# Rotating the queries feature-major in two PSUM banks, in a two-layer trunk

## Chip, core and metric

One core of a Trainium2 chip runs the whole program. The metric is the device time of one execution in microseconds (us); the median of several runs counts.

## What is computed

A trunk of two layers on 512 positions and 1024 features, all fp32: a pooling mixer, then multi-head latent attention, then a final norm. The change lies in the second layer. Cut to that:

```
def apply_rope(t, cos, sin):
    half = QK_ROPE_DIM // 2                      # 32
    t1, t2 = t[..., :half], t[..., half:]
    return concatenate([t1 * cos - t2 * sin, t2 * cos + t1 * sin], axis=-1)

def mla_layer(...):                              # 16 heads
    proj = rmsnorm(x, norm_g) @ w_in             # q_lat 384, kv_lat 256, k_rope 64, z 2048
    q = (rmsnorm(q_lat, q_norm_g) @ w_q_b).reshape(B, S, 16, 192)
    q_nope, q_rope = q[..., :128], q[..., 128:]
    kv = (rmsnorm(kv_lat, kv_norm_g) @ w_kv_b).reshape(B, S, 16, 256)
    k_nope, v = kv[..., :128], kv[..., 128:]
    q_rope, k_rope = apply_rope(q_rope), apply_rope(k_rope)
    s = q_nope . k_nope + q_rope . k_rope        # causal, scaled
    y = (softmax(s) @ v).reshape(B, S, 2048) * silu(z)
    return x + y @ w_out
```

## The kernel before, in words

Products are made from three matmuls (`mm3`, lines 181 to 184): each operand is kept as a rounded half `hi` and a remainder `lo`. ACT copies into `hi`, DVE or POOL subtracts for `lo` (`halves`, line 186; `Strip.split`, line 164, for weights). Weights come through five `raw` buffers by transfers that SP issues (lines 154 and 160), are split, and stay in four large or two small strips. PSUM has eight banks, taken by `bank()`.

Attention runs over 16 heads. The queries' rotary part is made for four heads at a time, a *part*, by the class `QRope` (line 700). For one part, `a(t)` makes 128 positions: nine matmuls of 256 columns (positions on the partitions), the rotation by `rope` (line 645: four DVE instructions) and `halves` into `qs`, hi and lo side by side. `b(t)` turns that with four PE transposes (line 728), so that features lie on the partitions, and ACT copies it into `q_r` (line 733). The four `a` and `b` of a part are spread out by hand: part 0 between the gate projections (`gates`, line 739), the later ones one per head (lines 954 to 977).

A head's iteration (line 952) has, in order: `scores(h + 1)` (line 857), the transposes of head h's probabilities (line 900), the softmax of h + 1, two of the projection units of the next pair of heads (line 797: `k` and `q`, each with a copy of its first 128 positions at line 817), `b`, `values(h)` (line 915), `a`, and after an odd head the two `v` units. In scores, `q_r` is multiplied with `k_a` and `k_b` (lines 869, 870), the other part of query and key by `mm3`, for the first block in one fp32 matmul (line 872) that takes the copies `q` and `k` of line 817. DVE takes the maxima `mx` (line 876), scales them to `nm` (line 889), ACT makes the exponentials (line 892), DVE the reciprocal and the scaling (lines 895, 898). The program is not issued as written: a scheduler orders each engine's queue by the order in the program and by what it takes to be ready, except in the stages marked `manual_schedule`.

"Head h" below is the stretch on PE that begins with the transposes of head h; the scores at its end are those of h + 2. Its rows start at 569.83 us for head 8, 580.69 for head 9 and 594.55 for head 10.

Of the kernel before, what the change touches and what calls it, by code (L numbers as in the profile page):

```python
# [11 lines left out]
F32 = mybir.dt.float32  # L12
F32R = mybir.dt.float32r
I32 = mybir.dt.int32
AF = mybir.ActivationFunctionType
# [35 lines left out]
def trunk_kernel(  # L51
# [20 lines left out]
    def f32(ap):  # L72
        return ap.bitcast(F32)
# [19 lines left out]
    def bank(dtype=F32):  # L93
        return ps.tile([P, 512], dtype, name="bank", tag="bank")
# [75 lines left out]
    def strip(parts, eng=dve, small=False):  # L170
        st = Strip(parts, small=small)
        st.split(st.pieces, eng)
        return st.views
# [12 lines left out]
    def halves(src, hi, lo):  # L186
        act.activation(hi, src, AF.Copy)  # L187
        dve.tensor_tensor(lo, src, f32(hi), ALU.subtract)
# [456 lines left out]
    def rope(src, t, nh):  # L645
        shape = [P, nh, DR]
        hf = DR // 2
        o = lp.tile([P, 4, DR], F32, name="rope_o", tag="rope", bufs=3)[:, :nh, :]
        q = lp.tile([P, 4, DR], F32, name="rope_q", tag="rope", bufs=3)[:, :nh, :]
        cb = cs2[:, t, :].unsqueeze(1).to_broadcast(shape)  # L650
        dve.tensor_tensor(o, src, cb, ALU.mult)
        for a, b in ((0, hf), (hf, 0)):
            sb = sn2[:, t, a : a + hf].unsqueeze(1).to_broadcast([P, nh, hf])
            dve.tensor_tensor(q[:, :, a : a + hf], src[:, :, b : b + hf], sb, ALU.mult)
        dve.tensor_tensor(o, o, q, ALU.add)
        return o

    def latents():
        for t in range(NT):
            for c0, c in ((0, QR), (QR, KVR)):  # L660
                v = lat[:, t, c0 : c0 + c]
                junk = lp.tile([P, QR], F32, name="junk", tag="t2", bufs=2)
                rs = inv_rms(v, junk[:, :c], c)
                dve.tensor_scalar(v, v, rs, None, ALU.mult)

# [10 lines left out]

    def k_rope_a(t):
        o = rope(lat[:, t, QR + KVR :].unsqueeze(1), t, 1)
        kh = lt.tile([P, 2, DR], F32R, name="kh", tag="kr", bufs=8)
        kl = lt.tile([P, 2, DR], F32R, name="kl", tag="kr", bufs=8)  # L680
        halves(o.to_broadcast([P, 2, DR]), kh, kl)
        return kh, kl

# [13 lines left out]

    q_r = {}

    class QRope:  # L700


        def __init__(self, part):
            (self.wv,) = strip([(w_q[:, :, 4 * part : 4 * part + 4, DN:], 3, 256)], eng=pool, small=True)
            home = lp if part == 0 else wk
            self.out = home.tile([P, 4, S], F32R, name="q_r", tag="q_r", bufs=1 + (part > 0))
            q_r[part] = self.out
            self.q = {}

        def a(self, t):  # L710
            b = bank()[:, :256]
            for k in range(3):
                mm3(
                    b,
                    tuple(v[:, k, t * P : (t + 1) * P] for v in (latT_hi, latT_lo)),
                    tuple(v[:, k, :] for v in self.wv),
                    k == 0,
                    k == 2,
                )
            o = rope(b.rearrange("p (h c) -> p h c", h=4), t, 4)  # L720
            q = lp.tile([P, 4, 2, DR], F32R, name="qs", tag="t2", bufs=2)
            halves(o, q[:, :, 0, :], q[:, :, 1, :])
            self.q[t] = q

        def b(self, t):
            b = bank(F32R)
            for i in range(4):
                pe.transpose(  # L728
                    b[:, i * P : (i + 1) * P],
                    self.q[t][:, i].rearrange("p a c -> p (a c)"),  # L730
                    identr,
                )
            act.activation(
                self.out[:, :, t * P : (t + 1) * P],
                f32(b).rearrange("p (h c) -> p h c", h=4),
                AF.Copy,
            )

    def gates(s, between=()):
        (wv,) = strip([(w_cols(w_in2, LAT + s * 256, 256), KD, 256)])  # L740
# [7 lines left out]
    latents()  # L748
    gates(0)
    lat_rows()  # L750
    kk = [k_rope_a(t) for t in range(NT)]
    gates(1)
    k_rope_b(kk)
    qr = QRope(0)
    gates(2, [lambda: qr.a(0), lambda: qr.a(1)])
    qr.b(0)
    gates(3, [lambda: qr.a(2), lambda: qr.a(3)])
    qr.b(1)
    gates(4, [lambda: qr.b(2), lambda: qr.b(3)])
    for i in range(5, 8):  # L760
        gates(i)


# [174 lines left out]
    qr = {1: QRope(1)}  # L938
    k0()
    q0()  # L940
    qr[1].a(0)
    k1()
    sc = scores(0)
    softmax(*sc)
    q1()
    qr[1].a(1)
    for u in vs:
        u()
    qr[1].b(0)
    units = projections(1)  # L950
    fill = {12: [(0, 0)], 13: [(0, 1)], 14: [(1, 0), (1, 1)], 15: [(2, 0), (2, 1)]}
    for h in range(H):
        p, odd = divmod(h, 2)
        g, t = divmod(h + 6, 4)
        gb, tb = divmod(h + 5, 4)
        if h == min(fill):
            o2.load(0, y_late)
        nxt = scores(h + 1) if h + 1 < H else None
# [9 lines left out]
        for i, (t_, n) in enumerate(fill.get(h, ())):  # L968
            for j in range(2):
                o2.block(0, t_, n, j)  # L970
        if h < 11:
            qr[gb].b(tb)
        values(h)
        if g < 4:
            if t == 0:
                qr[g] = QRope(g)
            qr[g].a(t)
        if odd:
            for u in units[2]:
                u()  # L980
# [16 lines left out]
        ap.tile([P, D], F32, name="o", tag=tag, bufs=n)  # L997
        for tag, n in (("pm", 2), ("pm", 2), ("pt_hi", 1), ("pt_lo", 1))
    ]
    junk = lp.tile([P, 512], F32, name="junk", tag="t2", bufs=2)  # L1000
    ssq = {t: [] for t in range(NT)}
    rs = {}
    lefts, rights = slice(0, 512), slice(512, D)
# [109 lines left out]
```

## Time and profile before

| | |
|---|---|
| median of 3 runs | 743.92 us (742.78 to 744.31) |
| profiled execution | 742.62 us, span 740.8 us |
| PE | 726.3 us busy (98%), granted clock 0.997 |
| DVE, ACT, POOL | 386.2 (52%), 326.8 (44%), 95.3 us (13%) |
| transfers | 28.2% of 16 engines' span on SP's queue, 63.06 MB |

Busy times can overlap between engines and say nothing alone of what waits for what. A matmul's duration is a model and overlaps the next one's, so the distance between two starts tells what one costs. "Idle before" in brackets is the time an engine stood still ahead of an instruction, with what ended it.

### The profile page before, as it was taken

To read this page: it belongs to the slowest core of one execution; us is meant where nothing else is said; L and a number is where in the kernel's file an instruction comes from. 1 tells how busy PE (TensorE), PEld (TensorE's weight loads), DVE (VectorE), ACT (ScalarE), POOL (GpSimd) and SP (SyncE) were. 2 spreads that over 40 slices of the span, in tenths; PEclk is the share of its full clock that TensorE was granted. 3 is DMA by queue.
4 is the path that set the end of the run, shared out by engine and by line. 5 is a ranking of instruction groups with operands and counts; after the bars stand their busy time and mean duration, and the time that the engine had idled before them with its cause. 6 is when DMAs were issued, how large, how long until landed. Compare 5 with 4: busy or idle time off the path is not lost.

```text
span 740.8 us, 10219 instructions
## 1 busy us (share of the span) xinstructions
PE 726.3 (98%) x3747; PEld 622.4 (84%) x3747; DVE 386.2 (52%) x824; ACT 326.8 (44%) x749; POOL 95.3 (13%) x141
## 2 busy tenths in 40 slices
PE   7999999999999999999999999999999999999995
PEld 6888888888888888889888888989898989888884
DVE  5954444544655323271633312767776767744325
ACT  6552332322324322254633334675666565623314
POOL 5000000000000000234500014230232020000006
PEclk9999999999999999999999999999999999999998
DMA  7433233233233223224432313120121021113203
GB/s 258 127 116 95 76 114 98 75 112 114 71 100 114 88 85 109 70 78 112 136 102 58 108 51 113 37 77 10 37 86 48 4 71 58 58 58 114 82 19 113
DMA packets 58914, 63.91 MB, mean 86 GB/s; under 512 B 10736, under 2 KB 44656, under 8 KB 58864
## 3 DMA queue, kind: packets, MB, share of 16 engines
q1 hardware_dynamic: 58720, 63.06, 28.2%
q8 instruction: 29, 0.48, 0.3%
q14 instruction: 21, 0.17, 0.1%
q10 hardware_dynamic: 144, 0.20, 0.1%
HBM read 61.15 MB, written 2.10 MB: 85 GB/s over the span
## 4 chain that ended last, share of the span: by engine, by line
PE 94%; DVE 2%; ACT 1%; POOL 1%; issue 1%; DMA 0%; POOLq 0%; SPq 0%; ACTq 0%
PE bank L182 28%; PE bank L184 28%; PE bank L183 28%; PE bank L906 2%; PE bank L300 2%; PE bank L869 1%; PE bank L870 1%; DVE xn L217 1%; PE bank L728 1%; PE bank L872 1%; PE bank L928 0%; DMA xs<-in_x 0%; ACT xn L197 0%; DVE xs L572 0%; PE bank L270 0%
## 5 line engine op out<-in xcount | busy, mean ns | idle before, releaser
L166 ACT ACTIVATE w_hi<-raw 128x512 fp32r<-128x512 f32 (+2 forms) x240 | 127.4, 584 | 192.3 <-PE bank L183 181.4
L167 DVE TENSOR_TENSOR w_lo<-raw,w_hi 128x512 fp32r<-128x512 f32 x172 | 112.1, 690 | 171.8 <-ACT w_hi L166 169.9
L182 PE MATMUL bank<-h_hi,w_hi 128*128 128x512 f32 x368 | 143.7, 391 | 0.0
L184 PE MATMUL bank<-h_lo,w_hi 128*128 128x512 f32 x368 | 143.3, 389 | 0.0
L183 PE MATMUL bank<-h_hi,w_lo 128*128 128x512 f32 x368 | 143.2, 389 | 0.0
L167 POOL TENSOR_TENSOR w_lo<-raw,w_hi 128x256 fp32r<-128x256 f32 (+2 forms) x68 | 62.3, 946 | 311.0 <-ACT w_hi L166 310.8
L184 PEld LDWEIGHTS bank<-h_lo,w_hi 128*128 128x128 f32 x368 | 69.1, 188 | 14.4
L183 PEld LDWEIGHTS bank<-h_hi,w_lo 128*128 128x128 f32 x368 | 69.1, 188 | 14.1
L182 PEld LDWEIGHTS bank<-h_hi,w_hi 128*128 128x128 f32 x368 | 69.1, 188 | 14.1
L182 PE MATMUL bank<-w_hi,yh 128*128 128x512 f32 x128 | 49.9, 390 | 0.0
L184 PE MATMUL bank<-w_lo,yh 128*128 128x512 f32 x128 | 49.8, 389 | 0.0
L183 PE MATMUL bank<-w_hi,yl 128*128 128x512 f32 x128 | 49.8, 389 | 0.0
L876 DVE CUSTOM_DVE_ANT_0 pm<-bank,mask 128x128 f32<-128x128 f32 (+2 forms) x64 | 30.5, 490 | 15.8 <-PE bank L184 11.8
L892 ACT ACTIVATE pm<-pm,nm 128x128 f32<-128x128 f32 (+1 forms) x64 | 35.5, 564 | 1.8 <-DVE nm L889 1.3
L182 PE MATMUL bank<-w_hi,latT_hi 128*128 128x256 f32 x112 | 32.6, 291 | 0.0
L182 PE MATMUL bank<-latT_hi,w_hi 128*128 128x512 f32 x80 | 32.5, 406 | 0.0
L184 PE MATMUL bank<-w_lo,latT_hi 128*128 128x256 f32 x112 | 31.6, 282 | 0.0
L183 PE MATMUL bank<-w_hi,latT_lo 128*128 128x256 f32 x112 | 31.6, 282 | 0.0
L184 PE MATMUL bank<-latT_lo,w_hi 128*128 128x512 f32 x80 | 31.4, 392 | 0.0
L183 PE MATMUL bank<-latT_hi,w_lo 128*128 128x512 f32 x80 | 31.2, 390 | 0.0
L187 ACT ACTIVATE pt_hi<-bank 128x512 fp32r<-128x512 f32 (+2 forms) x48 | 20.0, 490 | 23.6 <-PE bank L906 23.6
L184 PEld LDWEIGHTS bank<-w_lo,yh 128*128 128x128 f32 x128 | 24.0, 188 | 5.0
(202 smaller groups left out, 1434.0 us busy)
## 6 DMA issues: line engine op xcount, KB each, us to landing
raw<-in_pool_w_in SPq DMA_DIRECT2D x64, 256.0 KB, 3.2
raw<-in_pool_w_out SPq DMA_DIRECT2D x32, 256.0 KB, 3.2
raw<-in_mla_w_in SPq DMA_DIRECT2D x32, 256.0 KB, 3.0
raw<-in_mla_w_out SPq DMA_DIRECT2D x32, 256.0 KB, 3.3
raw<-in_mla_w_q_b SPq DMA_DIRECT2D x36, 128.0 KB, 2.4
raw<-in_pool_w_group SPq DMA_DIRECT2D x16, 256.0 KB, 2.6
raw<-in_mla_w_kv_b SPq DMA_DIRECT2D x16, 256.0 KB, 3.0
raw<-in_mla_w_in SPq DMA_DIRECT2D x16, 176.0 KB, 2.7
```

Of the source, the lines that this page charges most:

```text
L166: act.activation(hi, raw, AF.Copy)
L167: ins = eng.tensor_tensor(lo, raw, f32(hi), ALU.subtract)
L182: pe.matmul(o, a[0], b[0], start=start, stop=False)
L183: pe.matmul(o, a[1], b[0], start=False, stop=False)
L184: pe.matmul(o, a[0], b[1], start=False, stop=stop)
L187: act.activation(hi, src, AF.Copy)
L217: dve.scalar_tensor_tensor(xn, xs[:, t, :], rs, g, ALU.mult, ALU.mult)
L300: pe.matmul(first[i][:, c], w0.views[0][a][:, k, i * P : (i + 1) * P], (h_hi, h_lo)[b][:, k, c], start=k == 0 and n == 0, stop=k == KD - 1 ...
L728: pe.transpose(b[:, i * P : (i + 1) * P], self.q[t][:, i].rearrange("p a c -> p (a c)"), identr,)
L876: dve.tensor_tensor_reduce(out=pm[:, OFF[i] : OFF[i] + w], in0=o[:, :w], in1=mask[:, S - w :], scale=1.0, scalar=-3.0e38, op0=ALU.add, op1 ...
L892: act.activation(v, v, AF.Exp, bias=nm[:, i : i + 1], scale=SCALE, accum_out=l[:, i : i + 1])
L906: pe.transpose(b[:, n : n + P], pm[:, OFF[i] + j * P : OFF[i] + (j + 1) * P], ident)
```

## The change

A part is now made feature-major. The weights' columns are put in the order half (2), head (4), feature (32) when they are split, the product `half(a)` has these columns as the stationary side and all 512 positions as the moving side, so one bank holds the first rotary half of four heads, another the second. `turn` rotates between the two banks with tables `cosT` and `sinT` (made once: two POOL copies, eight PE transposes, two ACT copies) and splits into `stack`. Sixteen transfers of 32 partitions x 512 put each head's four pieces (two halves, hi and lo) below one another in `q_r`. The transposes and ACT copies of `b` are gone. Part 0 has its halves in `gates(2)` and turns after it; part g = 1, 2, 3 has half 0 before head 0 or in heads 3 and 7, and half 1 and the turn in heads 0, 4 and 8. Several tiles have fewer buffers.

```diff
@@ -645,8 +645,8 @@
     def rope(src, t, nh):
         shape = [P, nh, DR]
         hf = DR // 2
-        o = lp.tile([P, 4, DR], F32, name="rope_o", tag="rope", bufs=3)[:, :nh, :]
-        q = lp.tile([P, 4, DR], F32, name="rope_q", tag="rope", bufs=3)[:, :nh, :]
+        o = lp.tile([P, 4, DR], F32, name="rope_o", tag="turned", bufs=1)[:, :nh, :]
+        q = lp.tile([P, 4, DR], F32, name="rope_q", tag="rope", bufs=1)[:, :nh, :]
         cb = cs2[:, t, :].unsqueeze(1).to_broadcast(shape)
         dve.tensor_tensor(o, src, cb, ALU.mult)
         for a, b in ((0, hf), (hf, 0)):
@@ -659,7 +659,7 @@
         for t in range(NT):
             for c0, c in ((0, QR), (QR, KVR)):
                 v = lat[:, t, c0 : c0 + c]
-                junk = lp.tile([P, QR], F32, name="junk", tag="t2", bufs=2)
+                junk = lp.tile([P, QR], F32, name="junk", tag="t2", bufs=1)
                 rs = inv_rms(v, junk[:, :c], c)
                 dve.tensor_scalar(v, v, rs, None, ALU.mult)
 
@@ -676,8 +676,7 @@
 
     def k_rope_a(t):
         o = rope(lat[:, t, QR + KVR :].unsqueeze(1), t, 1)
-        kh = lt.tile([P, 2, DR], F32R, name="kh", tag="kr", bufs=8)
-        kl = lt.tile([P, 2, DR], F32R, name="kl", tag="kr", bufs=8)
+        kh, kl = kr[:, 2 * t], kr[:, 2 * t + 1]
         halves(o.to_broadcast([P, 2, DR]), kh, kl)
         return kh, kl
 
@@ -697,44 +696,81 @@
 
     q_r = {}
 
+    cosT = lp.tile([P, S], F32, name="cosT")
+    sinT = lp.tile([P, S], F32, name="sinT")
+
+    def turned_tables():
+
+        four = lp.tile([P, 2, NT, 4, DR // 2], F32, name="four", tag="t2", bufs=1)
+        for i, (src, dst) in enumerate(
+            ((cs2[:, :, : DR // 2], cosT), (sn2[:, :, DR // 2 :], sinT))
+        ):
+            pool.tensor_copy(
+                four[:, i], src.unsqueeze(2).to_broadcast([P, NT, 4, DR // 2])
+            )
+            b = bank()
+            for t in range(NT):
+                pe.transpose(
+                    b[:, t * P : (t + 1) * P],
+                    four[:, i, t].rearrange("p h f -> p (h f)"),
+                    ident,
+                )
+            act.activation(dst, b, AF.Copy)
+
     class QRope:
 
 
         def __init__(self, part):
-            (self.wv,) = strip([(w_q[:, :, 4 * part : 4 * part + 4, DN:], 3, 256)], eng=pool, small=True)
-            home = lp if part == 0 else wk
-            self.out = home.tile([P, 4, S], F32R, name="q_r", tag="q_r", bufs=1 + (part > 0))
+            st = Strip([(w_q[:, :, 4 * part : 4 * part + 4, DN:], 3, 256)], small=True)
+
+            order = dict(a=2, h=4)
+            pieces = [
+                (
+                    raw[:, 0].rearrange("p (h a f) -> p h a f", **order),
+                    hi[:, 0].rearrange("p (a h f) -> p h a f", **order),
+                    lo[:, 0].rearrange("p (a h f) -> p h a f", **order),
+                )
+                for raw, hi, lo in st.pieces
+            ]
+            st.split(pieces, pool)
+            (self.wv,) = st.views
+            home = wk if part % 2 else lp
+            self.out = home.tile([P, 4, S], F32R, name="q_r", tag="q_r", bufs=1)
             q_r[part] = self.out
-            self.q = {}
-
-        def a(self, t):
-            b = bank()[:, :256]
+            self.banks = []
+
+        def half(self, a):
+            b = bank()
             for k in range(3):
                 mm3(
                     b,
-                    tuple(v[:, k, t * P : (t + 1) * P] for v in (latT_hi, latT_lo)),
-                    tuple(v[:, k, :] for v in self.wv),
+                    tuple(v[:, k, a * P : (a + 1) * P] for v in self.wv),
+                    tuple(v[:, k, :] for v in (latT_hi, latT_lo)),
                     k == 0,
                     k == 2,
                 )
-            o = rope(b.rearrange("p (h c) -> p h c", h=4), t, 4)
-            q = lp.tile([P, 4, 2, DR], F32R, name="qs", tag="t2", bufs=2)
-            halves(o, q[:, :, 0, :], q[:, :, 1, :])
-            self.q[t] = q
-
-        def b(self, t):
-            b = bank(F32R)
+            self.banks.append(b)
+
+        def turn(self):
+            one, two = self.banks
+            stack = lp.tile([P, 4, S], F32R, name="stack", tag="t2", bufs=1)
+            for n in range(2):
+                c = slice(n * 256, (n + 1) * 256)
+                o = lp.tile([P, 2, 256], F32, name="turned", tag="turned", bufs=1)
+                for i, (x, z, op) in enumerate(
+                    ((one, two, ALU.subtract), (two, one, ALU.add))
+                ):
+                    q = lp.tile([P, 256], F32, name="crossed", tag="rope", bufs=1)
+                    dve.tensor_tensor(o[:, i, :], x[:, c], cosT[:, c], ALU.mult)
+                    dve.tensor_tensor(q, z[:, c], sinT[:, c], ALU.mult)
+                    dve.tensor_tensor(o[:, i, :], o[:, i, :], q, op)
+                halves(o, stack[:, :2, c], stack[:, 2:, c])
             for i in range(4):
-                pe.transpose(
-                    b[:, i * P : (i + 1) * P],
-                    self.q[t][:, i].rearrange("p a c -> p (a c)"),
-                    identr,
-                )
-            act.activation(
-                self.out[:, :, t * P : (t + 1) * P],
-                f32(b).rearrange("p (h c) -> p h c", h=4),
-                AF.Copy,
-            )
+                for j in range(4):
+                    nc.sync.dma_start(
+                        f32(self.out[j * 32 : (j + 1) * 32, i, :]),
+                        f32(stack[i * 32 : (i + 1) * 32, j, :]),
+                    )
 
     def gates(s, between=()):
         (wv,) = strip([(w_cols(w_in2, LAT + s * 256, 256), KD, 256)])
@@ -748,16 +784,15 @@
     latents()
     gates(0)
     lat_rows()
+    kr = xn_tile(F32R).rearrange("p (n a c) -> p n a c", n=2 * NT, a=2)
     kk = [k_rope_a(t) for t in range(NT)]
+    turned_tables()
     gates(1)
     k_rope_b(kk)
     qr = QRope(0)
-    gates(2, [lambda: qr.a(0), lambda: qr.a(1)])
-    qr.b(0)
-    gates(3, [lambda: qr.a(2), lambda: qr.a(3)])
-    qr.b(1)
-    gates(4, [lambda: qr.b(2), lambda: qr.b(3)])
-    for i in range(5, 8):
+    gates(2, [lambda: qr.half(0), lambda: qr.half(1)])
+    qr.turn()
+    for i in range(3, 8):
         gates(i)
 
 
@@ -938,21 +973,18 @@
     qr = {1: QRope(1)}
     k0()
     q0()
-    qr[1].a(0)
     k1()
     sc = scores(0)
     softmax(*sc)
     q1()
-    qr[1].a(1)
+    qr[1].half(0)
     for u in vs:
         u()
-    qr[1].b(0)
     units = projections(1)
     fill = {12: [(0, 0)], 13: [(0, 1)], 14: [(1, 0), (1, 1)], 15: [(2, 0), (2, 1)]}
     for h in range(H):
         p, odd = divmod(h, 2)
-        g, t = divmod(h + 6, 4)
-        gb, tb = divmod(h + 5, 4)
+        g, t = divmod(h + 5, 4)
         if h == min(fill):
             o2.load(0, y_late)
         nxt = scores(h + 1) if h + 1 < H else None
@@ -968,13 +1000,13 @@
         for i, (t_, n) in enumerate(fill.get(h, ())):
             for j in range(2):
                 o2.block(0, t_, n, j)
-        if h < 11:
-            qr[gb].b(tb)
         values(h)
-        if g < 4:
+        if g < 4 and t < 2:
             if t == 0:
                 qr[g] = QRope(g)
-            qr[g].a(t)
+            qr[g].half(t)
+            if t == 1:
+                qr[g].turn()
         if odd:
             for u in units[2]:
                 u()
@@ -997,7 +1029,7 @@
         ap.tile([P, D], F32, name="o", tag=tag, bufs=n)
         for tag, n in (("pm", 2), ("pm", 2), ("pt_hi", 1), ("pt_lo", 1))
     ]
-    junk = lp.tile([P, 512], F32, name="junk", tag="t2", bufs=2)
+    junk = lp.tile([P, 512], F32, name="junk", tag="t2", bufs=1)
     ssq = {t: [] for t in range(NT)}
     rs = {}
     lefts, rights = slice(0, 512), slice(512, D)
```

On SP's queue the sixteen transfers of each part (line 770 of the changed kernel, `q_r<-stack`) stand among the loads of raw weights, which they used not to. From the first head on:

```order
+L770 DMA q_r<-stack 32x512 x16
+L154 DMA raw<-in_mla_w_q_b 128x4x64 x3
+L154 DMA raw<-in_mla_w_q_b 128x2x128 x3
+L160 DMA raw<-in_mla_w_kv_b 128x512 x2
+L154 DMA raw<-in_mla_w_q_b 128x2x128 x3
+L160 DMA raw<-in_mla_w_kv_b 128x512 x2
+L770 DMA q_r<-stack 32x512 x16
```

The `128x4x64` loads, the weights of the next part, come directly behind a part's transfers.

On PE, the end of head 2 (last matmul of its values, line 928, then scores of head 4). In the kernel before, from the last three matmuls of an `a` on:

```order
L182 MATMUL bank<-w_hi,latT_hi 128x256
L183 MATMUL bank<-w_hi,latT_lo 128x256
L184 MATMUL bank<-w_lo,latT_hi 128x256
L869 MATMUL bank<-k_a,q_r 128x256
L870 MATMUL bank<-k_b,q_r 128x256
L872 MATMUL bank<-k_4293,q_4309 128x128
L869 MATMUL bank<-k_a,q_r 128x384
L870 MATMUL bank<-k_b,q_r 128x384
L182 MATMUL bank<-kh,qh 128x384
```

In the changed one (lines 904, 905 and 907 are 869, 870 and 872 of before), where values and scores are adjacent:

```order
L963 MATMUL bank<-pt_3651,v_4155 128x128
L904 MATMUL bank<-k_a,q_r 128x256
L905 MATMUL bank<-k_b,q_r 128x256
L904 MATMUL bank<-k_a,q_r 128x384
L905 MATMUL bank<-k_b,q_r 128x384
L182 MATMUL bank<-kh,qh 128x384
L907 MATMUL bank<-k_4227,q_4243 128x128
L183 MATMUL bank<-kh,ql 128x384
```

Three matmuls of the third block moved ahead of the one that takes the copy `q`; heads 6 and 10 read the same.

On DVE, around a turn, at the end of head 4 and the start of head 5 (lines 764 to 766 are the rotation, line 911 the maxima, line 924 `nm`). In the changed kernel:

```order
L765 TENSOR_TENSOR crossed<-bank,sinT 128x256
L188 TENSOR_TENSOR stack<-turned,stack 128x2x256
L911 ISA pm,mx<-bank,mask 128x512
L911 ISA mx 128x1
L764 TENSOR_TENSOR turned<-bank,cosT 128x256 x2
L766 TENSOR_TENSOR turned<-turned,crossed 128x256
L188 TENSOR_TENSOR pt_lo<-bank,pt_hi 128x512
L765 TENSOR_TENSOR crossed<-bank,sinT 128x256
L188 TENSOR_TENSOR pt_lo<-bank,pt_hi 128x384
L766 TENSOR_TENSOR turned<-turned,crossed 128x256
L188 TENSOR_TENSOR pt_lo<-bank,pt_hi 128x256
L924 TENSOR_SCALAR nm<-mx 128x4
```

In other heads, as in all of them before, `nm` follows the last `mx` directly and the three `pt_lo` follow `nm`; here five rotation instructions stand between.

## Rows read from the trace of the kernel before

**Rows 1.** The page: the span, then busy time of each engine.
```profile
span 740.8 us, 10219 instructions
...
PE 726.3 (98%) x3747; PEld 622.4 (84%) x3747; DVE 386.2 (52%) x824; ACT 326.8 (44%) x749; POOL 95.3 (13%) x141
```
**Rows 2.** The page: the chain that ended last, by engine.
```profile
PE 94%; DVE 2%; ACT 1%; POOL 1%; issue 1%; DMA 0%; POOLq 0%; SPq 0%; ACTq 0%
```
**Rows 3.** PE's waits: engine, line, waited for: us in total, times, longest.
```profile
PE bank L872 <- ACT q L817: 0.4, 1, 0.4
```
**Rows 4.** PE's timeline in the gate projections: start, us, what.
```profile
386.26 0.28 PE L182 MATMUL bank<-w_hi,latT_hi 128*128 128x256 f32 x1
...
387.34 0.40 PE L182 MATMUL bank<-h_hi,w_hi 128*128 128x512 f32 x1
...
392.81 0.28 PE L182 MATMUL bank<-w_hi,latT_hi 128*128 128x256 f32 x1
...
393.88 0.45 PE L728 MATMUL bank<-identr,qs 128*128 128x128 f32 x4
394.17 0.46 PE L182 MATMUL bank<-h_hi,w_hi 128*128 128x512 f32 x1
394.47 0.40 PE L183 MATMUL bank<-h_hi,w_lo 128*128 128x512 f32 x1
```
**Rows 5.** DVE's timeline, last scaling of latents; the chain, their transposes.
```profile
362.87 0.35 DVE L664 TENSOR_SCALAR lat<-lat,rs 128x256 f32<-128x256 f32 x1 [0.46 <-POOL rs L203]
...
367.12 2.19 PE bank L670 x20
```
**Rows 6.** Timeline of head 8, to the first row of head 9.
```profile
569.83 1.25 PE L906 MATMUL bank<-ident,pm 128*128 128x128 f32 x10
...
577.16 0.28 ACT L817 ACTIVATE q<-bank 128x128 f32<-128x128 f32 x1 [0.19 <-DVE ql L188]
...
577.60 0.28 PE L869 MATMUL bank<-k_a,q_r 128*128 128x256 f32 x1
...
577.84 0.39 PE L872 MATMUL bank<-k,q 128*128 128x128 f32 x2
...
580.69 1.25 PE L906 MATMUL bank<-ident,pm 128*128 128x128 f32 x10
```
**Rows 7.** Timeline of head 10.
```profile
594.55 1.25 PE L906 MATMUL bank<-ident,pm 128*128 128x128 f32 x10
...
601.18 0.36 PE L869 MATMUL bank<-k_a,q_r 128*128 128x256 f32 x1
...
601.89 0.28 ACT L817 ACTIVATE q<-bank 128x128 f32<-128x128 f32 x1 [0.19 <-DVE ql L188]
...
602.22 0.49 PE L872 MATMUL bank<-k,q 128*128 128x128 f32 x2 [0.38 <-ACT q L817]
```
**Rows 8.** Timeline of head 9.
```profile
587.59 0.28 ACT L817 ACTIVATE q<-bank 128x128 f32<-128x128 f32 x1 [0.19 <-DVE ql L188]
...
591.56 0.39 PE L872 MATMUL bank<-k,q 128*128 128x128 f32 x2
```
**Rows 9.** DVE groups (count, busy, mean ns of one); head 9's `pt_lo` in the timeline.
```profile
L651 DVE TENSOR_TENSOR rope_o<-bank,cs 128x256 f32<-128x256 f32 x16 | 6.8, 425 | 11.2 <-PE bank L184 11.0
...
L188 DVE TENSOR_TENSOR yl<-y,yh 128x512 fp32r<-128x512 f32 x16 | 10.9, 689 | 13.9 <-ACT yh L187 13.8
...
L876 DVE CUSTOM_DVE_ANT_0 pm<-bank,mask 128x128 f32<-128x128 f32 (+2 forms) x64 | 30.5, 490 | 15.8 <-PE bank L184 11.8
...
582.01 1.49 DVE L188 TENSOR_TENSOR pt_lo<-bank,pt_hi 128x512 fp32r<-128x512 f32 x3 [0.22 <-ACT pt_hi L187]
```
**Rows 10.** SP's first four loads; their landing; issue times of lines 160's loads.
```profile
0.72 1.81 SPq L104 DMA_DIRECT2D xs<-in_x  x4
...
DMA to landing us min/median/max: 2.7/3.4/4.4
...
L160 SPq DMA_DIRECT2D raw<-in_pool_w_in x64: 367/368/1519, 3.1 to 194.2; - x64
```

## The prediction

> **What bounds the kernel now.** I read the page's totals first: TensorE (PE) is busy 726.3 of 740.8 us; no other engine passes 52% [rows 1]. The chain that ended last says the same as a path: 94% of it is PE [rows 2]. So PE's instruction stream is the time, and any matmul taken off it is worth its own pitch, unless PE then reaches something that isn't ready. The list of PE's waits shows one such place in the attention: 0.4 us for the copy `q` (line 817) [rows 3]. What matters is therefore two numbers: what PE no longer executes, and how much of that was covering the DVE-ACT chain behind `q`.
>
> **Pitches.** Durations of matmuls overlap, so I take starts. One `a(t)`, nine matmuls of 256 columns, lasts from 386.26 to 387.34: 1.08 us. The 24 matmuls of 512 columns after it, 387.34 to 392.81, have a pitch of 0.228 us. One `b(t)`, four transposes, lasts from 393.88 to 394.17, and the matmul behind it starts its successor 0.30 instead of 0.23 later: 0.29 + 0.07 = 0.36 us [rows 4]. Twenty fp32 transposes take 2.19 us, 0.11 each [rows 5].
>
> **The change on PE.** Removed: 16 x 1.08 = 17.3 and 16 x 0.36 = 5.8, together 23.1 us. Added: 8 halves of nine 512-column matmuls, 72 x 0.228 = 16.4 us; 8 transposes for the two tables, 0.9 + 0.07 = 0.95 us. Net -5.7 us. Note that the halves alone give only 17.3 - 16.4 = 0.9: the gain is mostly the transposes.
>
> **What the removed work covered.** In an even head PE runs transposes, two projection units, (`b`), values, (`a`), and then the scores of a new pair, whose first block needs `q`. Head 8 has `a` and `b`: ACT starts the copy 577.16 - 569.83 = 7.33 us after the transposes begin, PE uses it at 577.84, 8.01 us after them [rows 6]. Head 10 has no `a`: the copy starts 601.89 - 594.55 = 7.34 us after, the same, and PE, which had begun the scores at 601.18, gets through at 602.22, 7.67 us after, having waited [rows 7]. So the DVE-ACT chain takes 7.67 us whatever PE does. Before the change head 8 was 0.34 us slower than that. In heads 2 and 6 the change takes away `a` and `b` and puts no half there: 1.44 us less work, of which 0.34 shortens the head. The order (second fence) brings three more matmuls of 384 columns ahead of the wait, 1.5 x 0.12 = 0.18 each, 0.5 us. The rest, 1.44 - 0.34 - 0.5 = 0.6 us, becomes waiting: +1.2 us for the two heads (bounds 0, if the chain shortens, and 2.9, if nothing is recovered). Head 10 loses `b` (0.36) and gets two more matmuls moved up (0.35): 0. Heads 0, 4 and 8 have half 1 there, nine matmuls at 0.228 = 2.05 us for the 1.44 taken: more cover than before, 0. Odd heads have the v units between: in head 9 `q` is copied at 587.59 and used at 591.56 [rows 8], 3.7 us after the copy's end, against 1.44 us lost: 0. The first scores lose the cover of one `a`: 0.1 us (0 to 1.08).
>
> **The turn on DVE.** Per part DVE had sixteen rotation instructions and four splits; now twelve of 128x256 and two splits of 128x512. The nearest rows are 0.43 and 0.69 us [rows 9], so 12 x 0.43 + 2 x 0.69 = 6.5 us, in one lump in heads 0, 4 and 8 and the start of the next. The order (third fence) has the last `pt_lo` behind nearly all of it. From half 1's end DVE must do twelve rotation steps less the one done earlier (4.7), one split (0.7), the four maxima (4 x 0.49 = 2.0) and the three `pt_lo` (1.5) [rows 9]: 8.9 us. PE meanwhile does scores (580.69 - 577.60 = 3.1 [rows 6]), transposes 1.0, units 15 x 0.23 = 3.5 and 1.4 of values before it needs the last `pt_lo`: 9.0 us. Even. I take +0.1 us for each of three heads (0, as back-to-back DVE instructions overlap a little, to 0.6, if hand-overs to ACT add up): +0.3 us. The softmax behind it starts some 4 us late, but the odd head's PE work until its transposes is 12 us. For part 0 the gate projections that follow cover all of it. ACT's 16 removed `q_r` copies only lighten ACT. One of the tables' POOL copies goes ahead of the last `pow` of the latents; those were scaled by 363.2 and PE transposes them at 367.1 [rows 5], so the copy would have to take over 3.9 us to be seen. ACT's and POOL's splits of these weights now write runs of 32 columns, still some heads ahead of the halves; `rope`, `junk` and `kh` with fewer buffers change order, not work. All of these: 0, and if that cover were gone, at most what each step lasts, under 1 us apiece.
>
> **The transfers.** Each part now issues 16 transfers of 64 KB on SP, ahead of the next raw weights. No row shows one within SBUF. The nearest are the four first loads: 1.81 us to issue four, 0.45 us each, while each takes 2.7 to 4.4 us to land [rows 10]; so transfers overlap in the queue. Then 16 take 16 x 0.45 = 7.2 us to issue. Counted from the transposes of the odd head after a turn, the stack is ready at about 6.5 us, issuing ends at 13.7, and the three raws behind land by 13.7 + 1.4 + 3.4 = 18.5 us. ACT wants the first after the `q` copy of the following even head: head 9 lasts 594.55 - 580.69 = 13.9 [rows 6, 7], less 1.44, plus 7.6, so at 20 us. `q_r` itself is needed from about 19 us on, and its first four transfers land at 6.5 + 1.8 + 4.4 = 12.7. Both hidden: 0, with a cover of 1.5 and 6 us. If that cover is gone, ACT stands still in order, with exps queued behind.
>
> The Trainium skill speaks against this part: "DMA: Bandwidth & Descriptors", section Bandwidth, says to batch transfers to 1 MiB and calls those under 64 KB dominated by their descriptors, and its section "Anatomy of one DMA" fits a fixed cost near 2 us to each (measured on POOL's queue). By an estimate from that page, paid one after another, 16 would take over 32 us. The trace agrees that a landing takes over 2 us, and not that it is paid in turn, since the four first loads were issued within 1.81 us.
>
> **Sum.** -5.7 + 1.2 + 0.1 + 0.3 = -4.1 us. The profiled execution took 742.62 us (span 740.8 [rows 1] and 1.8 around it); the sum makes 738.5 of it. The median of the runs shown is 743.92, 1.3 above that execution, so the forecast for a median is **739.8 us**.
>
> **Rivals.**
> 1. *Everything is covered*: the chain behind `q` shortens, since DVE and ACT lose work too, and no wait appears. -5.7: 738.2 us. For it: 16 copies and 16 small splits leave ACT. Against: head 10's chain was as long as head 8's although it had one rotation less [rows 6, 7]. Chance 0.16.
> 2. *The cover is used up*: heads 2 and 6 lose all 1.44, three turns cost 0.6 each, the first scores 1.08: 5.8 us of waits against 5.7 of gain. About 743.5, no change. The two banks that a turn holds over a head work the same way, if PE must wait for one. Against: the scheduled order leaves DVE and PE level, not behind. Chance 0.15.
> 3. *Slower, by the queue*: the transfers hold SP. ACT loses nothing until the raws come 3 us later than ACT wants them, when the next transposes' copies are due at 23 us: that is, from (23 - 6.5 - 4.8)/16 = 0.73 us per transfer on. At 1.5 us each, the longest that one issue took here [rows 10], the raws come at 6.5 + 24 + 4.8 = 35 us, 12 us late, in two heads: +24 - 4 = +20, 764 us. Against: issues took 0.37 us at the median [rows 10]. By the Trainium skill, "DMA: Bandwidth & Descriptors", section Bandwidth, it would land here or later; no row bears that out. Chance 0.07.
> 4. *It doesn't do what it says*: if the halves ran at the pitch of two 256-column matmuls, 0.24, they would give 0.0 instead of 0.9, and the sum would be -3.2; this lies inside the forecast's range and gets no chance of its own.
>
> **How the numbers follow.** Forecast (739.0 to 741.5): 0.62. A measurement of this kernel can tell about 0.2%, 1.5 us, from no change. Faster by more than that, under 742.4: the forecast, rival 1 and a fifth of rival 2, 0.62 + 0.16 + 0.03 = 0.81. Within: the rest of rival 2, 0.12. Slower: rival 3, 0.07. Range: down to rival 1's 738.2 with half a microsecond of the median's spread, 737.8; up through most of rival 2, to 743.2.
>
> **What would show it.** Right: PE busy near 726.3 - 5.7 = 720.6; the group of half's matmuls at a pitch of 0.23; two or three waits of PE for the copy `q`, 0.4 to 0.7 us each, one of them old; rotation steps near 0.43 us; `q_r` transfers issued at 0.5 us or less and landing in 2 to 4.5 us; no PE wait on a DMA. Wrong: ACT waiting over 2 us on a raw `in_mla_w_q_b` (rival 3), PE waiting on `pt_lo`, `mx` or a bank in heads 1, 5 and 9 (rival 2), no new wait at all (rival 1).

## The result and the profile after

The changed kernel takes 739.71 us (median of 4 runs, 738.48 to 740.2), the kernel before 744.12 beside it (4 runs); the ratio is 0.9941 with a 95% interval of 0.9923 to 0.996. Faster, by 4.4 us. On another chip the same pair gave 738.7 and 743.3 us, 0.9942 (0.9929 to 0.9954).

The page after, first its totals, then the chain that ended last; they answer to [rows 1] and [rows 2].

```profile
span 738.2 us, 10030 instructions
...
PE 722.7 (98%) x3619; PEld 616.8 (84%) x3619; DVE 384.8 (52%) x800; ACT 318.9 (43%) x727; POOL 96.9 (13%) x143
...
PE 92%; DVE 4%; ACT 1%; POOL 1%; issue 1%; DMA 0%; POOLq 0%; SPq 0%; ACTq 0%
```

PE is busy 3.6 us less, and still the bound. The prediction said 5.7 less. Most of the difference is not in the change: from the transposes of the latents to the end, the stretch that holds all the changed work of PE, it is busy 365.37 us before and 359.87 after, 5.5 less. Ahead of that, between 10 and 20 us, PE's granted clock is lower than before, 0.71 of full speed as a mean between its levels of 1.2 and 2.4 GHz, after 10 us in which PE was busy for 5.35 (5.81 before). Why it was lower no run shows. The stretches of 10 us at the start of the two traces (length, then busy us and count of PE, PEld, DVE, ACT, POOL, then the granted clock); first before:

```profile
10.00:20.00 10.00, 9.33 (x73) 8.46 (x72) 8.90 (x18) 7.73 (x19) 6.84 (x12) 1.00 0.77 264
```

After:

```profile
10.00:20.00 10.00, 10.00 (x64) 9.65 (x63) 7.80 (x16) 6.14 (x14) 6.91 (x12) 0.71 0.78 265
```

The transposes of the latents, ahead of everything that was changed on PE, begin at 368.71 instead of 366.96 us. A second profile of the same changed kernel has a clock of 0.90 there, and the transposes at 366.68, so this start moves by 2 us from one execution to another. I therefore count from these transposes on. A head's length is the difference of two starts in PE's timeline.

| us | before | after | difference |
|---|---|---|---|
| latents' transposes to head 0 | 103.98 | 102.41 | -1.57 |
| heads 0, 4, 8 (lose `a`, `b`; get half 1) | 10.84 to 10.86 | 11.48 to 11.53 | +0.65 each |
| heads 1, 5, 9 (lose `a`, `b`) | 13.86 to 13.88 | 12.32 to 12.33 | -1.55 each |
| heads 2, 6 (lose `a`, `b`) | 10.86 | 10.27 | -0.59 each |
| heads 3, 7 (lose `a`, `b`; get half 0) | 13.86 | 14.49, 14.52 | +0.64 each |
| head 10 (loses `b`) | 10.57 | 10.26 | -0.31 |
| heads 0 to 10 | 134.18 | 131.29 | -2.89 |
| head 11 to the end | 135.68 | 135.79 | +0.1 |
| sum | 373.84 | 369.49 | -4.35 |

Where a head lost PE work and got none back it lost time, but heads 2 and 6 lost the least for what was taken. PE's waits after (line, what it waited for: us, times, longest; compare [rows 3]):

```profile
PE bank L270 <- DVE xn L263: 2.8, 2, 1.5
PE bank L127 <- POOL ident masks.py:199: 1.9, 1, 1.9
PE bank L907 <- ACT q L852: 1.6, 3, 0.5
PE bank L225 <- DVE xn L217: 1.2, 1, 1.2
```

The wait for the copy `q` stood once before; now it stands in heads 2, 6 and 10. Head 2 on PE: its transposes, the first block of scores, the wait, the next transposes.

```profile
494.95 1.25 PE L941 MATMUL bank<-ident,pm 128*128 128x128 f32 x10
...
501.18 0.36 PE L904 MATMUL bank<-k_a,q_r 128*128 128x256 f32 x1
...
502.70 0.49 PE L907 MATMUL bank<-k,q 128*128 128x128 f32 x2 [0.52 <-ACT q L852]
...
505.22 0.60 PE L941 MATMUL bank<-ident,pm 128*128 128x128 f32 x4
```

PE gets through 502.70 - 494.95 = 7.75 us after the head's start; it was 7.67 in head 10 before [rows 7]. What ACT does until then, from the last copies of the projections on:

```profile
499.65 0.58 ACT L187 ACTIVATE kh<-bank 128x512 fp32r<-128x512 f32 x1
500.13 0.49 ACT L187 ACTIVATE qh<-bank 128x384 fp32r<-128x384 f32 x1
501.91 0.28 ACT L852 ACTIVATE k<-bank 128x128 f32<-128x128 f32 x1 [1.29 <-DVE kl L188]
502.37 0.28 ACT L852 ACTIVATE q<-bank 128x128 f32<-128x128 f32 x1 [0.19 <-DVE ql L188]
502.89 0.75 ACT L166 ACTIVATE w_hi<-raw 128x256 fp32r<-128x256 f32 x2 [0.24 <-DMA raw<-in_mla_w_q_b]
```

Two things are to be seen. ACT stands still for 1.29 us before the copy `k`, until DVE has read `kl` from the same PSUM bank; the projected values were there all the time. And the raw weights behind the transfers come 0.24 us after ACT asks for them. SP's queue at that turn:

```profile
488.38 10.02 SPq L770 DMA_DIRECT2D q_r<-stack  x16
498.49 6.03 SPq L154 DMA_DIRECT2D raw<-in_mla_w_q_b  x6
```

and the page's line on all such transfers (count, size, median us to landing):

```profile
q_r<-stack SPq DMA_DIRECT2D x64, 64.0 KB, 2.0
```

On DVE, the rotation steps and the split (busy us, mean ns, idle before):

```profile
L765 DVE TENSOR_TENSOR crossed<-bank,sinT 128x256 f32<-128x256 f32 x16 | 6.7, 420 | 2.2 <-PE bank L184 2.1
L188 DVE TENSOR_TENSOR stack<-turned,stack 128x512 fp32r<-128x512 f32 x8 | 5.5, 693 | 2.5 <-ACT stack L187 2.5
```

### The profile page after: what moved, and what is told of

Its sections match the earlier page's. It is cut to its first block, busy times and chain, and to the rows that moved or that the text cites. A ratio compares the mean times of both kernels' runs of the same rounds, so it can differ in the third digit from the quotient of the medians.

```text
span 738.2 us, 10030 instructions
## 1 busy us (share of the span) xinstructions
PE 722.7 (98%) x3619; PEld 616.8 (84%) x3619; DVE 384.8 (52%) x800; ACT 318.9 (43%) x727; POOL 96.9 (13%) x143
## 4 chain that ended last, share of the span: by engine, by line
PE 92%; DVE 4%; ACT 1%; POOL 1%; issue 1%; DMA 0%; POOLq 0%; SPq 0%; ACTq 0%
PE bank L183 28%; PE bank L184 28%; PE bank L182 28%; PE bank L941 2%; PE bank L300 2%; PE bank L904 1%; PE bank L905 1%; DVE xn L217 1%; PE bank L907 1%; ACT pm L927 1%; DVE pm L933 1%; PE bank L270 1%; DVE nm L924 0%; DMA xs<-in_x 0%; ACT xn L197 0%
## 5 line engine op out<-in xcount | busy, mean ns | idle before, releaser
L182 PE MATMUL bank<-latT_hi,w_hi 128*128 128x512 f32 x104 | 42.3, 407 | 0.0
L184 PE MATMUL bank<-latT_lo,w_hi 128*128 128x512 f32 x104 | 40.7, 391 | 0.0
L183 PE MATMUL bank<-latT_hi,w_lo 128*128 128x512 f32 x104 | 40.7, 391 | 0.0
L182 PEld LDWEIGHTS bank<-w_hi,yh 128*128 128x128 f32 x128 | 24.0, 188 | 5.0
L183 PEld LDWEIGHTS bank<-w_hi,yl 128*128 128x128 f32 x128 | 24.0, 188 | 4.9
L184 PE MATMUL bank<-d_lo,w_hi 128*128 128x512 f32 x64 | 25.3, 395 | 0.0
```

Of the source, the lines that this page charges most:

```text
L182: pe.matmul(o, a[0], b[0], start=start, stop=False)
L183: pe.matmul(o, a[1], b[0], start=False, stop=False)
L184: pe.matmul(o, a[0], b[1], start=False, stop=stop)
```

## Experiments

The changed kernel was run once more, unedited, beside the edits:

> The changed kernel once more, unedited, on the chip of this group, so that the edits of half a per cent are compared with it as well as with the kernel before. By the theory, 739.7 us, three waits of PE for the copy q. Rival (the 739.71 was a chance of that chip): the ratio to the kernel before comes out over 0.997.

738.7 us, three waits of 1.5 us in all, and every stretch within 0.07 us of the first profile (table below). The ratio is 0.9942, so the rival (over 0.997) falls: the result holds on both chips.

All edits start from the changed kernel. Each was timed against the kernel before on its chip (743.51 us in the first group, 743.3 in the second). Stretches, as in the table above:

| us | to head 0 | heads 0 to 10 | rest | sum | time | ratio to before |
|---|---|---|---|---|---|---|
| after (first profile) | 102.41 | 131.29 | 135.79 | 369.49 | 739.71 | 0.9941 (0.9923 to 0.996) |
| after (again) | 102.42 | 131.22 | 135.78 | 369.42 | 738.7 | 0.9942 (0.9929 to 0.9954) |
| 1 transposes back | 104.37 | 135.56 | 135.82 | 375.75 | 745.59 | 1.0025 (1.0015 to 1.0036) |
| 2 work into the waits | 102.38 | 132.99 | 135.78 | 371.15 | 741.16 | 0.9964 (0.9952 to 0.9977) |
| 3 copies first | 102.26 | 130.10 | 135.68 | 368.04 | 737.59 | 0.9921 (0.9907 to 0.9934) |
| 4 half 0 earlier | 102.42 | 129.92 | 135.80 | 368.14 | 738.05 | 0.9926 (0.9913 to 0.9939) |
| 5 both | 102.27 | 129.56 | 135.67 | 367.50 | 736.67 | 0.9912 (0.9896 to 0.9927) |
| 6 transfers twice | 102.42 | 135.24 | 135.87 | 373.53 | 743.88 | 1.0008 (0.9997 to 1.0019) |
| 7 longer turn | 102.42 | 132.77 | 136.39 | 371.58 | 741.28 | 0.9974 (0.9965 to 0.9983) |

**1. The transposes put back.** Is the gain the transposes on PE, or what ACT and DVE lost?

```
+    def spare():
+        b = bank(F32R)
+        for i in range(4):
+            pe.transpose(b[:, i * P : (i + 1) * P], latT_hi[:, 0, i * P : (i + 1) * P], identr)
...
+        if h < 11:
+            spare()
         values(h)
```

(and five more calls among the gates and before head 0.)

> The changed kernel with unused work put back: sixteen groups of four 128x128 transposes into a bank that nothing reads, at the places where the kernel before had its transposes of q_r (four among the gates, one before the heads, one in each of heads 0 to 10). Theory (the gain is mostly the sixteen groups of transposes that PE no longer executes, 0.36 us each): 16 x 0.36 = 5.8 us more PE work, of which the groups in heads 2, 6 and 10 stand in the waits of 0.5 us and cost little: +4.7 us against the changed kernel, 744.4 us, no different from the kernel before. Rival (the gain comes from the work that ACT and DVE lost, the copies of q_r and the splits): +0 to +1 us, 740 to 741 us.

The time from the latents on grows by 375.75 - 369.49 = 6.3 us, more than the 4.7 expected: 0.39 us for each of the sixteen groups. A group costs the same ahead of head 0 (1.96 / 5) as in heads 0, 3, 4, 7 and 8 (0.37 to 0.42), and a little more in heads 1, 5 and 9 (0.44 to 0.49). Only heads 2, 6 and 10 pay less, 0.31 each, but not nothing: the waits stay at 1.3 us in all.

```profile
PE bank L916 <- ACT q L861: 1.3, 3, 0.4
```

The scheduler explains it: with more work ahead of the wait it puts fewer matmuls of the scores there (one of 384 columns where the changed kernel has three), so most of a group's 0.39 us is added behind. With the transposes in, the changed kernel is 0.25% slower than the kernel before, and the rival (+0 to +1 us) falls. So the whole gain is the transposes, and all the rest of the change together costs 6.3 - 4.35 = 1.9 us.

**2. Work into the waits.** Nine unused matmuls of 256 columns behind the values in heads 2, 6 and 10.

```
         values(h)
+        if h in (2, 6, 10):
+            b = bank()[:, :256]
+            for k in range(3):
+                mm3(
+                    b,
+                    tuple(v[:, k, :P] for v in (latT_hi, latT_lo)),
+                    tuple(v[:, k, :256] for v in (latT_hi, latT_lo)),
+                    k == 0,
+                    k == 2,
+                )
```

> The changed kernel with nine unused 256-column matmuls into a free bank added behind the values in heads 2, 6 and 10 alone, where a(t) stood before the change in heads 2 and 6: 3 x 1.08 = 3.24 us more PE work. Theory (in these heads the DVE-ACT chain behind q takes 7.7 us whatever PE does, and PE arrives 0.5 us early): the three waits vanish and the heads grow by 0.3 to 0.6 us only, as matmuls of the scores that were moved up stay behind; in all +1.0 to +1.7 us, 741.0 us. Rival (the waits are only a record of when PE looked; the work adds in full): +3.2 us, 742.9 us.

The three heads grow by 0.55 to 0.57 us for 1.08 us of work, +1.66 in the sum, and PE's list of waits has no copy `q` any more. PE really was idle there; half of the work was free. The rival (+3.2) falls.

**3. The copies first.** What makes the copy late: the whole chain, or its place behind the halves?

```
                 c0 = P if name == "q" else 0
-                halves(b[:, c0:], th[:, c0:], tl[:, c0:])
                 t0 = ap.tile([P, P], F32, name=f"{name}0", tag=f"{name}0", bufs=1)
                 act.activation(t0, b[:, :P], AF.Copy)
+                halves(b[:, c0:], th[:, c0:], tl[:, c0:])
```

> The changed kernel with one line moved: in the joined projection of k and q, the copy of columns 0 to 128 (k0, q0) is written ahead of the halves of columns 128 to 512 instead of behind them. Theory (the three waits of PE for the copy q, 0.5 us each, come from the copy standing on ACT behind the q half, and behind DVE's ql of the same bank): the copy starts right behind the bank's last matmul or the piece before it, some 0.5 us earlier, the waits of heads 2, 6 and 10 vanish or fall under 0.2 us each, those heads shorten by 0.3 to 0.5 us, in all about -1 us against the changed kernel: 738.7 us, ratio to the kernel before 0.993. Rival A (it is the DVE-ACT chain as a whole that is late): the copy gets done earlier, but the scores' next block then waits as long for qh or ql, heads keep their 10.27 us, time as the changed kernel. Rival B: k0 and q0 delay kh and qh for the even heads with cover too, +0.2 us a head, +1 us.

ACT in head 2, which begins at 494.15 here:

```profile
498.86 0.26 ACT L851 ACTIVATE k<-bank 128x128 f32<-128x128 f32 x1
499.02 0.59 ACT L187 ACTIVATE kh<-bank 128x512 fp32r<-128x512 f32 x1
499.50 0.28 ACT L851 ACTIVATE q<-bank 128x128 f32<-128x128 f32 x1
499.65 0.51 ACT L187 ACTIVATE qh<-bank 128x384 fp32r<-128x384 f32 x1
501.77 0.80 ACT L166 ACTIVATE w_hi<-raw 128x256 fp32r<-128x256 f32 x2 [1.61 <-DMA raw<-in_mla_w_q_b]
```

The copy `q` starts 499.50 - 494.15 = 5.35 us after the head's start, where it was 502.37 - 494.95 = 7.42: two microseconds earlier, from one line's place. These copies no longer wait for DVE. PE's waits for `q` are gone, heads 2, 6 and 10 shorten from 10.27 to 9.87, and no other head grows by more than 0.05, so rival B falls. The sum is 1.45 us lower, 737.59 us: the theory's size or a little more. Rival A holds in small. The list of PE's own waits has none left in the attention, but the list of its weight loads (PEld) has a new one, in heads 2, 6 and 10:

```profile
PEld bank L183 <- DVE ql L188: 0.9, 3, 0.3
```

The block of scores now stands 0.30 us a head for the next thing from DVE, `ql`. ACT now idles 1.61 us for the raw weights; the transposes' copies behind begin at 504.72 and still wait for PE before that, so this costs nothing.

The Trainium skill, "PSUM — Partial Sum Buffer", section "PSUM bank collisions raise a hardware error", says that two engines must not use the same partitions of one bank at the same time, reads against reads included. The trace agrees, in that this program keeps the two engines apart: `kl` ends at 501.88 and the copy `k` starts at 501.91. In the changed kernel ACT's waits have

```profile
ACT k L852 <- DVE kl L188: 13.3, 12, 1.5
```

and after the move not one such wait is left. No run here let the two collide.

**4. Half 0 earlier.** The same work, but the half that stood in heads 3 and 7 comes ahead of the scores in heads 2 and 6. The edit also asks for the weights of parts 2 and 3 earlier (in heads 0 and 4) and, in lines not shown, takes the tile of `q_r` in `turn`.

```
-        g, t = divmod(h + 5, 4)
+        g, t = {0: (1, 1), 2: (2, 0), 4: (2, 1), 6: (3, 0), 8: (3, 1)}.get(h, (4, 0))
...
-        if g < 4 and t < 2:
-            if t == 0:
-                qr[g] = QRope(g)
+        if h in (0, 4):
+            qr[h // 4 + 2] = QRope(h // 4 + 2)
+        if g < 4:
```

> The changed kernel with half 0 of parts 2 and 3 (nine 512-column matmuls, 2.05 us) placed in heads 2 and 6, ahead of the scores, where it stood in heads 3 and 7. Same work, other place. Theory (heads 2 and 6 wait 0.5 us each because nothing covers the DVE-ACT chain behind q there, and recover what the chain is long): the two waits vanish; heads 2 and 6 go from 10.27 to 11.5 to 11.7, the odd heads lose 2.05 us; together -1.0 to -1.5 us against the changed kernel: 738.4 us. The wait of head 10 stays (0.5). Rival A (the odd heads' length is set by something else than PE's work): heads 3 and 7 do not shorten by the whole 2.05 us, 0 us or up to +1. Rival B (the tile of the part's q_r, now taken later, or its stack's steps on DVE, delay the turn): a new PE wait on DVE in heads 3 to 5 and 7 to 9, +1 us.

Heads 2 and 6 are 11.62 us, heads 3 and 7 12.39: the pair takes 24.01 instead of 24.76 to 24.79. One wait is left, in head 10:

```profile
PE bank L908 <- ACT q L853: 0.5, 1, 0.5
```

The sum falls by 1.35 us, as expected, and neither rival shows: heads 3 and 7 shorten by the whole half, and PE has no new wait. The place of a piece of work on the bounding engine is worth 0.7 us a time, with not one instruction saved.

**5. Both edits.**

> The changed kernel with both edits: the copies of k0 and q0 ahead of the halves, and half 0 of parts 2 and 3 in heads 2 and 6. Theory (both edits take the same three waits away; without them PE has no wait left in the attention and its own work is the time): only the wait of head 10 comes on top of the second edit, 0.4 us: 737.6 us, the same as with the copies moved alone (737.59) within 0.5 us. Rival (each edit has a gain of its own): the two gains of 2.1 and 1.7 us add up, 736.0 us.

736.67 us, ratio 0.9912, the fastest of all, 2 us under the changed kernel (367.50 against 369.49). The gains of 1.45 and 1.35 do not add up to 2.8, since in the main they are the same waits; but both edits together are 0.54 us under the copies moved alone. The result lies between the theory (737.6, within 0.5) and the rival (736.0), and neither is right. Heads 2 and 3 take 24.00 us here and 9.87 + 14.49 = 24.36 there. These 0.36 us are found among the weight loads: with the copies moved alone, those of the scores in heads 2 and 6 still wait 0.30 us for `ql` and 0.33 for the maxima `mx`; with half 0 ahead of them, `ql` is no longer waited for there (one such wait is left, in head 10) and `mx` 0.18 us. So the theory's premise, that PE has no wait left once the copies are moved, was wrong: part of the waiting had gone from one list into the other.

**6. The transfers twice.** How much cover is left behind SP?

```
-            for i in range(4):
+            for i in (0, 0, 1, 1, 2, 2, 3, 3):
                 for j in range(4):
                     nc.sync.dma_start(
```

> The changed kernel with each transfer of the stack into q_r issued twice, 32 a part instead of 16; nothing else is changed. Theory (the 16 transfers hold SP for 10.3 us a part, and that just fits: ACT waits only 0.24 us for the raw weights behind them in head 2): SP is held 20 us, the raw weights land 10 us later, ACT stands in order, the next transposes' copies, due 3 us after, come 7 us late less the 1.4 to 1.8 us that PE can spare: PE waits 5 to 6 us in heads 3 and 7, +10 to +12 us against the changed kernel, 750 to 752 us. If a block of scores needs all of a part's transfers and not the four of its own head, PE waits some 10 us on q_r itself in heads 2, 6 and 10: +20 to +30 us. Rival (there is far more cover than the prediction's 1.5 and 6 us): 0 to +1 us.

SP's queue, and what PE meets in head 3:

```profile
486.65 21.38 SPq L770 DMA_DIRECT2D q_r<-stack  x32
508.07 4.14 SPq L154 DMA_DIRECT2D raw<-in_mla_w_q_b  x6
```

```profile
511.07 0.50 PE L182 MATMUL bank<-latT_hi,w_hi 128*128 128x512 f32 x1 [1.11 <-ACT w_hi L166]
511.87 0.50 PE L183 MATMUL bank<-latT_hi,w_lo 128*128 128x512 f32 x1 [0.30 <-POOL w_lo L167]
```

Slower by 4 us (373.53 against 369.45, the mean of the two profiles of the changed kernel), and the result is no faster than the kernel before. The rival falls: another 10 us on SP is not hidden. But the theory's 10 to 12 us falls too. The two heads that pay are 3 and 7, 16.46 and 16.50 instead of 14.5, 2.0 each, of which the two waits shown make 1.4 in head 3; and the wait is another one: not the transposes' copies behind a standing ACT, but half 0, whose weights are split late. The scheduler had moved ACT's split of these weights from ahead of the copies of head 3's transposes to behind its softmax, so ACT stood still there for 0.35 us at most. PE did not wait for `q_r` itself.

**7. A longer turn.** Is DVE level with PE in a turn, or does it have slack?

```
-                    dve.tensor_tensor(o[:, i, :], x[:, c], cosT[:, c], ALU.mult)
-                    dve.tensor_tensor(q, z[:, c], sinT[:, c], ALU.mult)
+                    for _ in range(2):
+                        dve.tensor_tensor(o[:, i, :], x[:, c], cosT[:, c], ALU.mult)
+                    for _ in range(2):
+                        dve.tensor_tensor(q, z[:, c], sinT[:, c], ALU.mult)
```

> The changed kernel with the eight multiplications of a turn issued twice each (the second writes the same values again): eight more DVE instructions of 128x256, 8 x 0.34 = 2.7 us more in one lump per part. Theory (the last pt_lo stands behind the turn on DVE and comes 1.4 us before PE wants it in heads 1, 5 and 9): PE waits 1.0 to 1.4 us for pt_lo in each, the transfers start 2.7 us later and ACT waits for the raw weights behind them in heads 2 and 6 about 2 us longer, still before the next transposes' copies: +3 to +4.2 us against the changed kernel, 743 us. Rival A (there is more slack on DVE): 0 us. Rival B (the prediction's own count, DVE and PE level, no slack): 2.7 us each, +8 us, 748 us.

+2.1 us in the sum, between the theory and rival A, and not where the theory put it. In heads 1, 5 and 9 PE waits for nothing: the scheduler moved v matmuls between those that take `pt_lo`. The wait comes later, at the transposes of heads 2, 6 and 10, for the scaling of the probabilities; PE's list of waits, and DVE at the first of them:

```profile
PE bank L943 <- DVE pm L935: 1.1, 3, 0.4
```

```profile
493.56 0.53 DVE L913 CUSTOM_DVE_ANT_0 pm<-bank,mask 128x384 f32<-128x384 f32 x1
494.01 0.08 DVE L913 DVE_READ_ACCUMULATOR2_ANT mx<- 128x1 f32 x1
494.01 2.22 DVE L935 TENSOR_SCALAR pm<-pm,l 128x128 f32<-128x128 f32 x4
```

Four such scalings took 1.28 us in the changed kernel. The three waits make 1.1 of the 2.1 us. The weight loads wait for `pm` six times, 3.0 us, so more of it may lie there; the order changed too (the last scores of a head now stand behind the first of the next transposes), and the rest stays open. The run bounds the price of this lump from above (2.7 us more on DVE cost 0.7 us a turn), and by that the prediction's 0.1 a turn was not too low; it doesn't give the slack itself, since the order changed with it.

## Why the prediction was right

It said 739.8 us; 739.71 and 738.7 were measured. That one of them agrees to 0.1 us is luck: the same kernel's medians on two chips differ by 1 us, and 738.7 lies under the 739.0 to 741.5 that the prediction called its forecast, though within its range. The difference is the better test: -4.1 predicted, -4.4 and -4.6 by the medians, -4.35 by the trace. Step by step:

- **PE's work, -5.7.** Right in kind and nearly in size (5.5 us less busy from the latents on). A half takes 2.04 us in the gates (388.89 to 390.93) for the 2.05 predicted, the tables' transposes 0.88 for 0.95. A group of `b` costs 0.39 instead of 0.36 by the first experiment, so the work removed is 0.5 us more. Rival 4 (256-column pitch) is out.
- **The chain behind `q`, +1.2 in heads 2 and 6.** The place is right, and the wait is 0.52 us for the 0.6 predicted. But the heads shortened by 0.59 and not by 0.84, so of the 1.44 taken each gave up 0.85: the term measures +1.7 and not +1.2. The chain was 7.75 instead of 7.67, and the three matmuls moved ahead of it brought 0.33 (2.52 us from the copy's use to the head's end, 2.85 in head 8 before [rows 6]), not 0.5. And "7.67 us whatever PE does" named the chain right but took it as given. More than a microsecond of it is ACT waiting for DVE to leave the bank. The third experiment removes that, and gains 0.40 us a head of it, since `ql` is the next thing that is late. The trace of before lists it too (ACT's copy `k` waits for DVE's `kl` 15 times, 10.5 us); I read only what PE waited for, not what the copy itself waited for.
- **Head 10, 0.** It lost 0.31 us of the 0.36 of its `b`: right, and its wait of 0.5 is the old one, a little longer.
- **First scores, +0.1.** No wait there. **Three turns, +0.3.** No wait; the last `pt_lo` is ready at 487.23 in head 1 and used at 488.59, 1.4 us of slack where "even" was predicted and 0.1 us a turn was put. Its count used 0.43 us a step, but steps that follow one another start 0.34 apart (479.72, 480.06, 480.39): twelve times 0.09 is 1.1 of the 1.4.
- **Transfers, hidden.** True, with less to spare than thought. Sixteen took 10.0 to 10.7 us to issue, 0.64 each, where 0.45 was taken from the four first loads [rows 10] and 0.5 or less was named as a sign of being right; they landed in 2.0 us at the median. The cover of 1.5 us to the raw weights is used up: ACT waits 0.24 to 0.34 us for them, at a moment when nothing behind it is due. Had rival 3's 0.73 us per transfer been reached, little would have happened, going by the sixth experiment: at twice the transfers the loss was 2.0 us a head, and not all the time beyond 3 us, because the order of ACT's queue isn't fixed.
- **The sum.** -4.1 predicted, -4.35 from the latents on. Ahead of head 0 my terms make -6 x 1.08 - 5 x 0.36 + 3 x 2.05 + 0.95 + 0.1 = -1.1, and -1.57 was measured; in heads 0 to 10 they make -3.0, and -2.89 was measured. The transposes' 0.03 and the tables explain 0.2 of the first, the wait that wasn't there 0.1; the last 0.2 stays open. That the heads' sum comes out so near is in part luck: the 0.5 us too little for heads 2 and 6 is made up by heads 1, 5 and 9, which lost 0.11 more each than the 1.44 counted, and by the turns, where heads 0, 4 and 8 grew by 0.65 and the work alone makes 0.61.

Rival 1 is out (the waits are there), rival 2 too (PE waits at no turn, and heads 2 and 6 lost 0.85 of their 1.44), and rival 3 does not come even with twice the transfers, which only take the gain back.

## What to carry to other kernels

On a kernel whose one engine is busy 98% of the span, count the instructions that the engine no longer executes, at pitches read from starts; then ask of each place that lost work what PE reaches next, and how long that takes regardless of PE. Where a wait of half a microsecond appears, look at the order of the queue of the engine that is waited for, as well as for cover: one line moved gave back 0.40 us in each of three heads, a half moved in front 0.75 in each of two. And read the waits of the weight loads beside those of the matmuls: a wait can leave the one list and go on in the other. Small transfers that replace transposes are free only as long as nothing due soon stands behind them in their queue.

## What I had not expected of the hardware

A tiny DVE instruction can last a microsecond. In head 2 of the changed kernel:

```profile
495.88 1.21 DVE L924 TENSOR_SCALAR nm<-mx 128x4 f32<-128x4 f32 x1
```

```profile
492.42 4.64 POOL L167 TENSOR_TENSOR w_lo<-raw,w_hi 128x256 fp32r<-128x256 f32 x5 [19.28 <-ACT w_hi L166]
```

`nm` has four columns and takes 0.17 us at the median of heads; here POOL is splitting weights until 497.06, and it takes 1.21. The 2.22 us of the four scalings in experiment 7 fall on such a stretch of POOL too (494.33 to 499.33). The Trainium skill, "SBUF — State Buffer", section "Who interferes with whom", says that DVE's second port pair is shared with GpSimd under an exclusive lock held for a whole instruction, and that a tensor-scalar operation can take that pair. The trace agrees: the extra 1.04 us is about one of POOL's instructions, 4.64 / 5 = 0.93, and `nm` ends at 497.09, just behind POOL's last at 497.06. In head 2 it delayed the exponentials by only 0.22 us, as ACT was busy with `pt_hi` until then; no run here removed it.

The start of the kernel was the other surprise: the same program had a granted clock of 0.71 from 10 to 20 us in one profile and 0.90 in another, and reached the latents 2 us later in the first. Differences of 2 us between two single executions of this kernel say nothing by themselves; stretches counted from a common point agree within 0.1 us.
